# Output projection of a short-convolution layer: the second 1024 columns together, four pairs by seven products, and the first gate on GpSimd

## The chip, the cores and the metric

One core of a Trainium2 chip runs the whole kernel. The metric is the device time of one execution in microseconds (us), the median of several runs. The engines are TensorE (PE; its weight loads are shown as PEld), VectorE (DVE), ScalarE (ACT), GpSimd (Pool) and SyncE (SP), which issues nearly all the loads.

## The reference, cut to what matters

One layer of a short gated convolution with a conditioned norm, in float32, over 256 tokens, a model width D of 2048 and a branch width E of 4096:

```python
h = rmsnorm(x, norm_g[layer])
h, gate = adaln(h, c, ada_w[layer], ada_b[layer])
proj = jnp.einsum('bsd,de->bse', h, w_in)
b_gate, c_gate, v, g = jnp.split(proj, 4, axis=-1)
u = causal_depthwise_conv(c_gate * v, conv_w)
y = b_gate * u * jax.nn.silu(g)
y = jnp.einsum('bse,ed->bsd', y, w_out)
x = x + gate[:, None, :] * y
return rmsnorm(x, final_g)
```

The change lies in the last three lines: y (256 x 4096) times W_out (4096 x 2048), the gated residual and the last norm, whose sum of squares runs over all 2048 columns.

## The kernel before

**Products.** Every float32 operand is split in a high part (rounded, a cast on ACT, `split_hi`, line 352) and a low part (the rest, a subtraction on DVE, `split_lo`, line 357). A product of two blocks is then three TensorE products, high by high, high by low and low by high: `triple` (line 720), 128x512 each in the output projection. The W_in products before it take the first four fifths of the time and are not touched.

**Tiles of the output projection.** y lies transposed: 32 channel tiles of 128 channels, in 16 pairs j, for two halves t of 128 tokens. W_out comes in slabs of 1 MB, `raw_o`, each a DMA issued by SP (`load_o`); three buffers each, used in turn, hold the loads and sums (tag lo), the high parts (tag hi) and the low parts (tag raw). So a load waits for the DVE operation that read the buffer last, and a cast for the PE products that read the high part three tiles ago.

**First 1024 columns.** A slab is two channel tiles (a pair) by 1024 columns. A plain slab takes eight block products for two channel tiles, two column halves and two token halves, 24 TensorE products. Six pairs (`SEVEN`, 10 to 15) take seven block products instead, 21, by sums of blocks: `seven` makes four sums of W_out blocks on DVE (lines 748 to 751), splits three raw blocks (749 and 752) and the four sums, and uses sums of token blocks that `token_forms` prepared. Plain and seven-pairs alternate in the list `order`. Three of the seven results go to extra banks (`p1`, `p6`, `p75`), which `gather` adds to tiles `ends` (called z in the profile); line 798 adds the banks of the plain results. Then `gated` (line 725) multiplies by the gate (731), adds x (732), squares and sums on ACT (733), and multiplies by the norm's weight (734): DVE and ACT alone. In the profile xr, the residual, and fg, the weight, are parts of the tile big.

**Last 1024 columns.** Two blocks of 512 columns (`dc` 2 and 3), each with eight slabs of four channel tiles by 512 columns, 24 products a slab. Block 2 ends in `gated`, and in the sum of squares so far, `part_sum`. For block 3 DVE multiplies the raw slab by the gate first (line 844), and x is put into the bank ahead (line 829), so that its bank ends as the final residual. The last three slabs of block 3 are done for t=0 first; t=1's 36 products of these slabs come last (`late`), so that `finish(0)` (square, root, reciprocal, scaling, four stores) runs beside them. `finish(1)` is the kernel's end. The two token halves of block 3 lie in two PSUM tiles (`both`).

**Order.** A scheduler places each engine's instructions by priorities and an estimate of time; each engine then runs its own list in that order, waiting on semaphores. An instruction that waits holds up all behind it on its engine.

Of the kernel before, what the change touches and what calls it, by code (L numbers as in the profile page):

```python
# [18 lines left out]
NCT = E // P  # L19
TT = T // P  # L20
EPS = 1e-6
# [9 lines left out]
SLOT = 2048  # L31
# [86 lines left out]
def short_conv_layer(ctx: ExitStack, tc: tile.TileContext, x, c, norm_g, ada_w, ada_b, w_in, conv_w, w_out, final_g, out):  # L118
    nc = tc.nc
# [11 lines left out]
    psum = ctx.enter_context(tc.tile_pool(name="psum", bufs=3, space=PSUM))  # L131
# [144 lines left out]
    for t in range(TT):  # L276
        for dh in range(2):
# [94 lines left out]
    def split(raw, n, lo_tag="lo"):  # L372

        return split_lo(raw, n, split_hi(raw, n), lo_tag)
# [22 lines left out]
    for k in range(KT):  # L397
        c_k = silu_c[:, k : k + 1]
        at, gv = first_ada[k], gv0
# [163 lines left out]
    whole = [0] * NCH  # L563
# [27 lines left out]
    def gate(dc):  # L591
        return gates[dc // 2][:, dc % 2, :]
# [35 lines left out]
    EP = 4  # L628
# [80 lines left out]
    LATE = 3  # L709

    def load_o(raw, e0, ne, c0, n):
        nc.sync.dma_start(
            raw.rearrange("p (k f) -> p k f", k=ne),
            w_out[0, e0 * P : (e0 + ne) * P, c0 : c0 + n].rearrange("(k p) f -> p k f", p=P),
        )

    def y_parts(ct, t):
        return [ys[ct // 2][:, ct % 2, h, t * P : (t + 1) * P] for h in range(2)]

    def triple(dst, y, hi, lo, opens=False, ends=False):  # L720

        for i, (a, b) in enumerate(((0, hi), (0, lo), (1, hi))):
            nc.tensor.matmul(dst, y[a], b, start=opens and i == 0, stop=ends and i == 2, skip_group_check=True)  # L723

    def gated(t, c0, n, src, pr, at):


        cs = slice(c0, c0 + n)
        r = xr[:, t, cs]
        g = gates[c0 // 1024].rearrange("p a f -> p (a f)")[:, c0 % 1024 : c0 % 1024 + n]  # L730
        nc.vector.tensor_tensor(out=pr, in0=src, in1=g, op=ALU.mult)
        nc.vector.tensor_tensor(out=r, in0=r, in1=pr, op=ALU.add)
        nc.scalar.activation(pr, r, AF.Square, scale=D**-0.5, accum_out=fsq[:, t, at : at + 1])
        nc.vector.tensor_tensor(out=r, in0=r, in1=fg[:, cs], op=ALU.mult)


    p75 = psum.tile([P, 2, W], F32, tag="mm", name="mm_7")
    wide = [psum.tile([P, 2, W], F32, tag="mm", name="mm_w") for _ in range(TT)]
    p1, p6 = (psum.tile([P, W], F32, tag="sm", name="mm_1", bufs=2) for _ in range(2))

    def seven(j, raw):


        opens, last = j == SEVEN[0], j == SEVEN[-1]
# [3 lines left out]
        nc.vector.tensor_tensor(out=s[:, 0:2], in0=b[:, 1:3], in1=b[:, 0:1].to_broadcast([P, 2, W]), op=ALU.subtract)  # L748
        nc.scalar.copy(bh[:, 1:4], b[:, 1:4])
        nc.vector.tensor_tensor(out=s[:, 2], in0=b[:, 2], in1=s[:, 0], op=ALU.add)  # L750
        all_sums = nc.vector.tensor_tensor(out=s[:, 3], in0=b[:, 3], in1=s[:, 2], op=ALU.subtract)
        low = nc.vector.tensor_tensor(out=bl[:, 1:4], in0=b[:, 1:4], in1=bh[:, 1:4].bitcast(F32), op=ALU.subtract)
# [7 lines left out]
        triple(wide[0][:, 1], y_parts(2 * j + 1, 0), bh[:, 3], bl[:, 3])  # L760
        triple(wide[0][:, 0], f(3), bh[:, 2], bl[:, 2])
# [3 lines left out]
        triple(wide[1][:, 1], y_parts(2 * j + 1, 1), sh[:, 3], sl[:, 3])  # L765

    def gather():
# [9 lines left out]
    order = (0, 1, 10, 2, 11, 3, 12, 4, 13, 5, 14, 6, 15, 7, 8, 9)  # L777
    for n, j in enumerate(order):
        raw = w_tile("lo" if n else "raw", "raw_o")
        load_o(raw, 2 * j, 2, 0, 2 * W)  # L780
        load_ends(n - 4)
        if j in SEVEN:
            seven(j, raw)
            if j == SEVEN[-1]:
                gather()
            continue
        hi, lo = split(raw, SLOT, "raw")
        for t in range(TT):
            for k in range(2):
                for d in range(2):  # L790
                    o = slice((k * 2 + d) * W, (k * 2 + d + 1) * W)
                    triple(
                        wide[t][:, d], y_parts(2 * j + k, t), hi[:, o], lo[:, o],
                        n == 0 and k == 0, j == order[-1] and k == 1,
                    )
    for t in range(TT):
        c = ends[t].rearrange("p h f -> p (h f)")
        nc.vector.tensor_tensor(out=c, in0=wide[t].rearrange("p h f -> p (h f)"), in1=c, op=ALU.add)
# [20 lines left out]
    n_ep = NCT // EP  # L819
    for dc in range(2, 4):  # L820
        dcs = slice(dc * W, (dc + 1) * W)
# [3 lines left out]
        late = []  # L825
        if dc == 3:

            for t in range(TT):
                nc.scalar.copy(po[t], xr[:, t, dcs])

        def out_mm(t, ep, hi, lo):
            for i in range(EP):
                ct = ep * EP + i
                o = slice(i * W, (i + 1) * W)
                triple(po[t], y_parts(ct, t), hi[:, o], lo[:, o], ct == 0 and dc < 3, ct == NCT - 1)

        for ep in range(n_ep):

            raw = w_tile("lo", "raw_o")
            load_o(raw, ep * EP, EP, dc * W, W)  # L840
            if dc == 3:

                raw3 = raw.rearrange("p (k f) -> p k f", k=EP)
                nc.vector.tensor_tensor(
                    out=raw3, in0=raw3, in1=gate(dc).unsqueeze(1).to_broadcast([P, EP, W]), op=ALU.mult
                )
            hi, lo = split(raw, SLOT, "raw")
            out_mm(0, ep, hi, lo)
            if dc == 3 and ep >= n_ep - LATE:
                late.append((ep, hi, lo))  # L850
            else:
                out_mm(1, ep, hi, lo)

        for t in range(TT):
            if t == 1:
                for ep, hi, lo in late:
                    out_mm(1, ep, hi, lo)
            pr = ends[t][:, 0]
            if dc == 2:
                gated(t, dc * W, W, po[t], pr, 1)  # L860
                ps = part_sum[:, t : t + 1]
                nc.vector.reduce_sum(ps, fsq[:, t, 0:2], axis=mybir.AxisListType.X)
                nc.vector.tensor_scalar_add(ps, ps, EPS)
            else:
                nc.scalar.activation(pr, po[t], AF.Square, scale=D**-0.5, accum_out=fsq[:, t, 2:3])
                finish(t)


# [22 lines left out]
```

## Time and profile before

| | us |
|---|---|
| median of 3 runs (lowest, highest) | 906.36 (906.14, 906.43) |
| profiled execution: its time | 907.4 |
| profiled execution: its span | 905.6 |
| first product of the output projection, from the span's start | 727.79 |
| last product's end | 898.01 |

Of the span PE is busy 98%, DVE 73%, ACT 53% and Pool 9%; Pool's work is the turning of gate sums during the W_in part, and nothing in the output projection. The profile is of one execution. A row of the timeline gives start, duration, engine, line, operation, output and inputs (buffer numbers left out), partitions x elements, count, and in brackets how long the engine was idle before and what released it. A row of a group gives the busy time and the mean of one in ns.

### The profile page before, as it was taken

To read this page: it belongs to the slowest core of one execution; us is meant where nothing else is said; L and a number is where in the kernel's file an instruction comes from. 1 tells how busy PE (TensorE), PEld (TensorE's weight loads), DVE (VectorE), ACT (ScalarE), POOL (GpSimd) and SP (SyncE) were. 2 spreads that over 40 slices of the span, in tenths; PEclk is the share of its full clock that TensorE was granted. 3 is DMA by queue.
4 is the path that set the end of the run, shared out by engine and by line. 5 is a ranking of instruction groups with operands and counts; after the bars stand their busy time and mean duration, and the time that the engine had idled before them with its cause. 6 is when DMAs were issued, how large, how long until landed. Compare 5 with 4: busy or idle time off the path is not lost.

```text
span 905.6 us, 16392 instructions
## 1 busy us (share of the span) xinstructions
PE 890.2 (98%) x7009; PEld 852.7 (94%) x7009; DVE 663.9 (73%) x643; ACT 477.8 (53%) x423; POOL 83.6 (9%) x95
## 2 busy tenths in 40 slices
PE   7899999999999999999999999999999999999996
PEld 4899999999999999999999999999999988888885
DVE  5789989988888866765965677565555578887882
ACT  6867866665548766644433444443444445544342
POOL 0000000000000133024224104320000000000000
PEclk9999999999999999999999999999999999999999
DMA  9999999999998588688887788776566486685542
GB/s 310 363 368 363 359 310 353 347 370 356 354 327 289 162 277 244 191 257 246 280 250 239 250 271 267 236 224 191 187 189 193 137 312 201 210 293 186 186 139 94
DMA packets 162665, 235.00 MB, mean 259 GB/s; under 512 B 6804, under 2 KB 105284, under 8 KB 162208
## 3 DMA queue, kind: packets, MB, share of 16 engines
q1 hardware_dynamic: 159456, 226.56, 76.3%
q0 software_dynamic: 3008, 7.34, 2.9%
q8 instruction: 55, 0.90, 0.4%
q14 instruction: 18, 0.15, 0.0%
q10 hardware_dynamic: 128, 0.04, 0.0%
HBM read 224.49 MB, written 2.10 MB: 250 GB/s over the span
## 4 chain that ended last, share of the span: by engine, by line
PE 93%; DMA 3%; SPq 1%; ACT 1%; issue 0%; DVE 0%; ACTq 0%
PE mm_b L491 38%; PE mm_s L491 36%; PE mm_o L723 10%; PE mm_w L723 7%; PE mm L723 2%; DMA at<-in_ada_w_dram 2%; DMA raw_s<-in_sc_w_in_dram 1%; SPq L231 1%; DMA x<-in_x_dram 1%; ACT hi L352 0%; PE tp_g L481 0%; ACT mm_s L524 0%; ACT acc L512 0%; SPq L460 0%; SPq L534 0%
## 5 line engine op out<-in xcount | busy, mean ns | idle before, releaser
L491 PE MATMUL mm_s<-hT,hi 128*128 128x256 f32 x2048 | 350.3, 277 | 1.6 <-ACT hT L328 0.9
L491 PE MATMUL mm_b<-hT,hi 128*128 128x256 f32 x2048 | 348.2, 276 | 0.0
L491 PEld LDWEIGHTS mm_s<-hT,hi 128*128 128x128 f32 x2048 | 308.3, 188 | 2.2 <-ACT hT L328 1.1
L491 PEld LDWEIGHTS mm_b<-hT,hi 128*128 128x128 f32 x2048 | 307.9, 188 | 0.0
L491 PE MATMUL mm_s<-hT,lo 128*128 128x256 f32 x1024 | 282.0, 277 | 0.9 <-DVE lo L357 0.8
L491 PE MATMUL mm_b<-hT,lo 128*128 128x256 f32 x1024 | 282.6, 276 | 0.0
L357 DVE TENSOR_TENSOR lo<-raw,hi 128x2048 fp32r<-128x2048 f32 (+1 forms) x66 | 154.0, 2334 | 101.1 <-ACT hi L352 100.8
L352 ACT CAST hi<-raw 128x2048 fp32r<-128x2048 f32 (+1 forms) x66 | 123.7, 1875 | 192.6 <-PE mm_b L491 150.0
L491 PEld LDWEIGHTS mm_s<-hT,lo 128*128 128x128 f32 x1024 | 191.7, 188 | 1.3 <-DVE lo L357 1.3
L491 PEld LDWEIGHTS mm_b<-hT,lo 128*128 128x128 f32 x1024 | 192.2, 188 | 0.0
L357 DVE TENSOR_TENSOR lo<-raw_s,hi 128x2048 fp32r<-128x2048 f32 (+1 forms) x80 | 149.7, 1877 | 40.2 <-ACT hi L352 39.7
L352 ACT CAST hi<-raw_s 128x2048 fp32r<-128x2048 f32 (+1 forms) x80 | 124.2, 1557 | 60.7 <-PE mm_s L491 49.7
L352 ACT CAST hi<-raw_o 128x2048 fp32r<-128x2048 f32 x26 | 49.6, 1907 | 68.2 <-PE mm_o L723 36.6
L474 DVE SCALAR_TENSOR_TENSOR gv<-at,silu_c,gv 128x512 f32<-128x512 f32 x105 | 78.5, 748 | 6.3 <-DMA at<-in_ada_w_dram 4.7
L357 DVE TENSOR_TENSOR lo<-raw_o,hi 128x2048 fp32r<-128x2048 f32 x26 | 59.5, 2289 | 30.1 <-ACT hi L352 30.1
L723 PE MATMUL mm_o<-hi,y 128*128 128x512 f32 x256 | 78.7, 389 | 0.0
L512 ACT COPY acc<-mm_s 128x1024 f32<-128x1024 f32 x54 | 54.6, 1012 | 39.4 <-PE mm_s L491 39.3
L723 PE MATMUL mm_w<-hi,y 128*128 128x512 f32 x184 | 58.8, 389 | 0.0
L723 PEld LDWEIGHTS mm_o<-hi,y 128*128 128x128 f32 x256 | 48.0, 188 | 9.9
L623 POOL TENSOR_TENSOR gacc<-gacc,z 128x512 f32<-128x512 f32 x28 | 44.0, 1572 | 109.1 <-DMA z<-gacc 109.1
L617 DVE SCALAR_TENSOR_TENSOR gacc<-at_g,silu_c,gacc 128x512 f32<-128x512 f32 x60 | 46.9, 781 | 5.9 <-DMA at_g<-in_ada_w_dram 4.7
L723 PE MATMUL mm_o<-lo,y 128*128 128x512 f32 x128 | 49.5, 389 | 0.0
(145 smaller groups left out, 579.4 us busy)
## 6 DMA issues: line engine op xcount, KB each, us to landing
raw<-in_sc_w_in_dram SPq DMA_DIRECT2D x64, 1024.0 KB, 5.8
raw_s<-in_sc_w_in_dram SPq DMA_DIRECT2D x47, 1024.0 KB, 8.1
raw_o<-in_sc_w_out_dram SPq DMA_DIRECT2D x32, 1024.0 KB, 5.3
at<-in_ada_w_dram SPq DMA_DIRECT2D x114, 256.0 KB, 8.0
raw_s<-in_sc_w_in_dram SPq DMA_DIRECT2D x33, 512.0 KB, 7.0
at_g<-in_ada_w_dram SPq DMA_DIRECT2D x32, 512.0 KB, 7.9
at<-in_ada_w_dram SPq DMA_DIRECT2D x6, 512.0 KB, 9.4
x<-in_x_dram SPq DMA_DIRECT2D x4, 512.0 KB, 6.1
```

The source lines that it names most:

```text
L231: nc.sync.dma_start(at[:, :, s, :], adas[:, j : j + kk, s, 0 : NK0 * P])
L352: nc.scalar.copy(hi[:, :n], raw[:, :n])
L357: nc.vector.tensor_tensor(out=lo[:, :n], in0=raw[:, :n], in1=hi[:, :n].bitcast(F32), op=ALU.subtract)
L474: nc.vector.scalar_tensor_tensor(out=gv, in0=at4[:, i], scalar=c_k, in1=gv, op0=ALU.mult, op1=ALU.add)
L491: mm = last_mm[0] = nc.tensor.matmul(dst, w, h[k], start=begins and left, stop=ends, skip_group_check=True)
L512: nc.scalar.copy(acc[ch, q], bank)
L617: nc.vector.scalar_tensor_tensor(out=ga, in0=at3[:, i, :], scalar=s, in1=ga, op0=ALU.mult, op1=ALU.add)
L623: nc.gpsimd.tensor_tensor(out=ga, in0=ga, in1=turned, op=ALU.add)
L723: nc.tensor.matmul(dst, y[a], b, start=opens and i == 0, stop=ends and i == 2, skip_group_check=True)
```

## The change

The second 1024 columns are done like the first: ten pairs in the order 0, 1, 10, 2, 11, 3, 12, 4, 13, 5, of which 10 to 13 by seven products (`columns`, the former loop as a function, called twice). The remaining twelve channel tiles (`LAST`, three slabs of four) are done one 512-column block at a time: first block 2, then block 3 with the gate multiplied into the slab as before, t=0 first and t=1's 36 products last. Between them the results of the pairs for block 3 are gated, added to x and put into the bank (ACT, line 855). Block 2's gate, squares and `part_sum` come after the last slab's split. The gate of the first 1024 columns runs on Pool instead of DVE. The two token halves of block 3 are the two halves of one PSUM tile, `p75` (mm_7 in the order), which held two of the seven results before.

```diff
-    def gated(t, c0, n, src, pr, at):
+    def gated(t, c0, n, src, pr, at, eng=nc.vector):
...
-        nc.vector.tensor_tensor(out=pr, in0=src, in1=g, op=ALU.mult)
-        nc.vector.tensor_tensor(out=r, in0=r, in1=pr, op=ALU.add)
+        eng.tensor_tensor(out=pr, in0=src, in1=g, op=ALU.mult)
+        eng.tensor_tensor(out=r, in0=r, in1=pr, op=ALU.add)
         nc.scalar.activation(pr, r, AF.Square, scale=D**-0.5, accum_out=fsq[:, t, at : at + 1])
-        nc.vector.tensor_tensor(out=r, in0=r, in1=fg[:, cs], op=ALU.mult)
...
+        eng.tensor_tensor(out=r, in0=r, in1=fg[:, cs], op=ALU.mult)
...
+            places = [(t, k, d) for t in range(TT) for k in range(2) for d in range(2)]
+            if n == 0 and c0:
+                places.sort(key=lambda p: p[2])
...
-        gated(t, 0, 2 * W, c, c, 0)
+        gated(t, 0, 2 * W, c, c, 0, nc.gpsimd)
...
-        both = [psum.tile([P, TT, W], F32, tag="mm", name="mm_o") for _ in range(1 + (dc == 3))]
-        po = [both[-t][:, t] for t in range(TT)]
...
+    halves = [wide_bank("mm_o") for _ in range(2)]
+    p75 = wide_bank("mm_7")
+    LAST = (3, 4, 7)
+    columns(
+        2 * W, (0, 1, 10, 2, 11, 3, 12, 4, 13, 5), SEVEN[0:4],
+        lambda t, d: halves[d][:, t], *extra_banks(), p75, False,
+    )
+    po = [p75[:, t] for t in range(TT)]
...
+    for ep in LAST:
+        raw = w_tile("lo", "raw_o")
+        load_o(raw, ep * EP, EP, 2 * W, W)
+        hi, lo = split(raw, SLOT, "raw")
         for t in range(TT):
...
+            out_mm(halves[0][:, t], t, ep, hi, lo)
+    for t in range(TT):
+        c = ends[t][:, 1]
+        nc.vector.tensor_tensor(out=c, in0=halves[1][:, t], in1=c, op=ALU.add)
+        nc.vector.tensor_tensor(out=c, in0=c, in1=gate(3), op=ALU.mult)
+        nc.vector.tensor_tensor(out=c, in0=c, in1=xr[:, t, 3 * W : 4 * W], op=ALU.add)
+        nc.scalar.copy(po[t], c)
+    late = []
+    for ep in LAST:
...
+        out_mm(po[0], 0, ep, hi, lo)
+        late.append((ep, hi, lo))
+    for t in range(TT):
+        c = ends[t][:, 0]
+        nc.vector.tensor_tensor(out=c, in0=halves[0][:, t], in1=c, op=ALU.add)
+        gated(t, 2 * W, W, c, c, 1)
...
+    for t in range(TT):
+        if t == 1:
+            for ep, hi, lo in late:
+                out_mm(po[1], 1, ep, hi, lo)
+        nc.scalar.activation(ends[t][:, 1], po[t], AF.Square, scale=D**-0.5, accum_out=fsq[:, t, 2:3])
+        finish(t)
```

ACT's queue at the start of the second 1024 columns, before: casts of the slabs of block 2 (hi from raw_o), the copies of x into the banks and the two squares of the first gate, whose input big DVE wrote.

```order
L352 CAST hi_8868<-raw_o_8866 128x2048
L352 CAST hi_8898<-raw_o_8896 128x2048
L352 CAST hi_8928<-raw_o_8926 128x2048
L829 COPY mm_o_9118<-big_8329 128x512
L829 COPY mm_o_9119<-big_8329 128x512
L352 CAST hi_8958<-raw_o_8956 128x2048
L733 ACTIVATE z0_4470,fsq_8330<-big_8329 128x1024
L733 ACTIVATE z1_4471,fsq_8330<-big_8329 128x1024
L352 CAST hi_8988<-raw_o_8986 128x2048
```

The same place now; hi_8872 and hi_8902 are pairs 0 and 1, hi_8933 and hi_8940 pair 10 (raw blocks, sums), hi_8967 pair 2, hi_8998 and hi_9005 pair 11, hi_9032 pair 3 and hi_9063 pair 12.

```order
L352 CAST hi_8872<-raw_o_8870 128x2048
L352 CAST hi_8902<-raw_o_8900 128x2048
L743 CAST hi_8933<-raw_o_8930 128x1536
L352 CAST hi_8940<-sums_o_8932 128x2048
L732 ACTIVATE z0_4470,fsq_8330<-big_8329 128x1024
L352 CAST hi_8967<-raw_o_8965 128x2048
L732 ACTIVATE z1_4471,fsq_8330<-big_8329 128x1024
L743 CAST hi_8998<-raw_o_8995 128x1536
L352 CAST hi_9005<-sums_o_8997 128x2048
```

The two squares (L732, of data that Pool writes) now stand one ahead of pair 2's cast and one between that and pair 11's first cast.

PE's queue between the seventh and the eighth slab of block 2, before: a slab's first product uses the high part, the second the low part.

```order
L723 MATMUL mm_o_8865<-hi_9048,y13_4465 128x512
L723 MATMUL mm_o_8865<-hi_9078,y14_4466 128x512
L723 MATMUL mm_o_8865<-lo_9080,y14_4466 128x512
L723 MATMUL mm_o_8865<-hi_9078,y14_4466 128x512 x2
L723 MATMUL mm_o_8865<-lo_9080,y14_4466 128x512
```

PE's queue now where pair 10 ends and pair 2 begins, with the semaphores that each row waits for:

```order
L722 MATMUL mm_o_8866<-lo_8942,y10_4462 128x512
L722 MATMUL mm_o_8866<-hi_8940,y10_4462 128x512
L722 MATMUL mm_o_8865<-hi_8967,y2_3606 128x512 [waits Activation_49]
L722 MATMUL mm_o_8866<-hi_8967,y2_3606 128x512
L722 MATMUL mm_1_8868<-hi_8998,y11_4463 128x512 [waits Activation_49]
L722 MATMUL mm_o_8865<-lo_8969,y2_3606 128x512 [waits DVE_49]
L722 MATMUL mm_o_8865<-hi_8967,y2_3606 128x512
```

A product with pair 11's high part (hi_8998) now stands ahead of all products with pair 2's low part (lo_8969).

PE's last products, before: t=0 ends in tile mm_o_9118 and t=1 goes on in mm_o_9119, without a wait.

```order
L723 MATMUL mm_o_9118<-hi_9318,y15_4467 128x512 x2
L723 MATMUL mm_o_9118<-lo_9320,y15_4467 128x512
L723 MATMUL mm_o_9118<-hi_9318,y15_4467 128x512
L723 MATMUL mm_o_9119<-hi_9299,y12_4464 128x512 x2
L723 MATMUL mm_o_9119<-lo_9301,y12_4464 128x512
L723 MATMUL mm_o_9119<-hi_9299,y12_4464 128x512
```

And now, where t=0's last slab (hi_9334) ends and the 36 products of t=1 begin:

```order
L722 MATMUL mm_7_8867<-hi_9334,y15_4467 128x512 x2
L722 MATMUL mm_7_8867<-lo_9336,y15_4467 128x512
L722 MATMUL mm_7_8867<-hi_9334,y15_4467 128x512
L722 MATMUL mm_7_8867<-hi_9296,y6_4444 128x512 [waits DVE_49]
L722 MATMUL mm_7_8867<-lo_9298,y6_4444 128x512
L722 MATMUL mm_7_8867<-hi_9296,y6_4444 128x512 x2
```

Both token halves are one tile here, and the first product of t=1 has a wait for DVE.

More of the change, by code (lines that the diff above doesn't have):

```diff
@@ L708, in short_conv_layer @@
     part_sum = const.tile([P, TT], F32, tag="part_sum", name="part_sum")
-    LATE = 3
     def load_o(raw, e0, ne, c0, n):
@@ L775, in gather, with columns, extra_banks, wide_bank @@
         add(ends[1][:, 0], p75[:, 1], ends[1][:, 1])
[L777 to L795, printed above, removed]
+    def columns(c0, order, sevens, bank, p1, p6, p75, whole, loads=None):
+        for n, j in enumerate(order):
+            raw = w_tile("raw" if n == 0 and c0 == 0 else "lo", "raw_o")
+            load_o(raw, 2 * j, 2, c0, 2 * W)
+            if loads:
+                loads(n - 4)
+            if j in sevens:
+                seven(j, raw, bank, p1, p6, p75, j == sevens[0], j == sevens[-1])
+                if j == sevens[-1]:
+                    gather(p1, p6, p75)
+                continue
+            hi, lo = split(raw, SLOT, "raw")
+            places = [(t, k, d) for t in range(TT) for k in range(2) for d in range(2)]
+            if n == 0 and c0:
+                places.sort(key=lambda p: p[2])
+            for t, k, d in places:
+                o = slice((k * 2 + d) * W, (k * 2 + d + 1) * W)
+                triple(
+                    bank(t, d), y_parts(2 * j + k, t), hi[:, o], lo[:, o],
+                    n == 0 and k == 0, j == order[-1] and k == 1 and (whole or d == 1),
+                )
+    def extra_banks():
+        return [psum.tile([P, W], F32, tag="sm", name="mm_1", bufs=2) for _ in range(2)]
+    def wide_bank(name):
+        return psum.tile([P, 2, W], F32, tag="mm", name=name)
+    p75 = wide_bank("mm_7")
+    wide = [wide_bank("mm_w") for _ in range(TT)]
+    columns(
+        0, (0, 1, 10, 2, 11, 3, 12, 4, 13, 5, 14, 6, 15, 7, 8, 9), SEVEN,
+        lambda t, d: wide[t][:, d], *extra_banks(), p75, True, load_ends,
+    )
     for t in range(TT):
@@ new lines, in short_conv_layer @@
+    late = []
+    for ep in LAST:
+        raw = w_tile("lo", "raw_o")
+        load_o(raw, ep * EP, EP, 3 * W, W)
+        raw3 = raw.rearrange("p (k f) -> p k f", k=EP)
+        nc.vector.tensor_tensor(out=raw3, in0=raw3, in1=gate(3).unsqueeze(1).to_broadcast([P, EP, W]), op=ALU.mult)
+        hi, lo = split(raw, SLOT, "raw")
+        out_mm(po[0], 0, ep, hi, lo)
[4 more added lines that the diff above has]
+        gated(t, 2 * W, W, c, c, 1)
+        ps = part_sum[:, t : t + 1]
+        nc.vector.reduce_sum(ps, fsq[:, t, 0:2], axis=mybir.AxisListType.X)
+        nc.vector.tensor_scalar_add(ps, ps, EPS)
```

60 lines of the change are left out of this document (13 added, 47 removed).

## The prediction

> **What bounds the kernel now.** I read the page first, then the chain of waits in order of time, then the busy time by stretch of the last part, then single instructions of VectorE (DVE), GpSimd (Pool) and ScalarE (ACT).
>
> ```profile
> PE 890.2 (98%) x7009; PEld 852.7 (94%) x7009; DVE 663.9 (73%) x643; ACT 477.8 (53%) x423; POOL 83.6 (9%) x95
> 794.16 16.79 PE mm_w L723 x74
> 810.96 87.05 PE mm_o L723 x384
> 898.03 0.70 ACT z L865 x2
> 760.00:780.00 20.00, 20.00 (x89) 16.54 (x89) 17.22 (x13) 9.75 (x6) 0.00 (x0) 1.00 0.65 205
> 860.00:880.00 20.00, 20.00 (x90) 16.57 (x89) 19.01 (x15) 8.25 (x6) 0.00 (x0) 1.00 0.49 157
> ```
>
> The first line is the page's engine table, the next three are the chain, the last two are busy time (PE, weight loads, DVE, ACT, Pool, then granted clock, DMA share, GB/s). PE is the bound and has no gap: the 384 products of the two column blocks that the change rewrites took 87.05 us, 226.7 ns each. A product removed there is worth 0.227 us, if PE is never made to wait. Behind PE stands DVE: 17.22 of 20 us while pairs by seven products alternate with plain pairs, so it has 2.8 us in 20 to spare.
>
> **Products.** Four pairs lose one group of three products each: 12 x 0.2267 = **-2.7 us**. This holds in any order; the order has 738 products after the W_in part instead of 750.
>
> **DVE work added and removed.** A seven-pair costs DVE these operations where a plain slab has the first alone:
>
> ```profile
> L357 DVE TENSOR_TENSOR lo<-raw_o,hi 128x2048 fp32r<-128x2048 f32 x5 | 11.5, 2292 | 7.1 <-ACT hi L352 7.1
> L752 DVE TENSOR_TENSOR lo<-raw_o,hi 128x1536 fp32r<-128x1536 f32 x5 | 8.8, 1751 | 0.0
> L748 DVE TENSOR_TENSOR sums_o<-raw_o 128x1024 f32<-128x1024 f32 x5 | 6.1, 1218 | 0.0
> L750 DVE TENSOR_TENSOR sums_o<-raw_o,sums_o 128x512 f32<-128x512 f32 x5 | 3.5, 692 | 0.2
> ```
>
> That is 1.22 + 2 x 0.69 + 1.75 + 2.29 = 6.6 us a pair. By itself it is hidden: the first 1024 columns run just so with PE full (the 760 to 780 row). The five gate multiplications fewer (eight slabs become three) free time that nobody waited for. Taking the six operations of the first gate off DVE gains nothing either: they stood beside plain slabs, which ask 2.29 us of DVE for every 24 products, 5.44 us, of PE. Cost zero, if DVE is not held up. It is, by the next edit.
>
> **First gate on Pool.** Six operations on 128x1024 go to Pool, at the moment when DVE gets its fullest stretch. The trace shows what a Pool operation does to a DVE operation that reads two SBUF tiles:
>
> ```profile
> 330.41 2.86 POOL L623 TENSOR_TENSOR gacc<-gacc,z 128x512 f32<-128x512 f32 x1 [5.63 <-DMA z<-gacc]
> 329.82 2.29 DVE L357 TENSOR_TENSOR lo<-raw_s,hi 128x2048 fp32r<-128x2048 f32 x1 [3.15 <-ACT hi L352]
> 332.55 2.87 DVE L357 TENSOR_TENSOR lo<-raw_s,hi 128x2048 fp32r<-128x2048 f32 x1 [0.44 <-ACT hi L352]
> 402.72 1.29 POOL L623 TENSOR_TENSOR gacc<-gacc,z 128x512 f32<-128x512 f32 x1 [5.88 <-DMA z<-gacc]
> 403.26 2.89 DVE L357 TENSOR_TENSOR lo<-raw,hi 128x2048 fp32r<-128x2048 f32 x1 [1.14 <-ACT hi L352]
> 488.49 1.30 POOL L623 TENSOR_TENSOR gacc<-gacc,z 128x512 f32<-128x512 f32 x1 [2.14 <-DMA z<-gacc]
> 488.47 0.69 DVE L677 TENSOR_TENSOR z<-mm_b,z 128x512 f32<-128x512 f32 x1 [1.32 <-PE mm_b L491]
> ```
>
> Pool's 512 elements take 1.29 us alone. Beside a DVE operation it took 2.86: that one ended at 332.11, and Pool 1.16 later, at 333.27. The next DVE operation, started at 332.55, took 2.87, 0.58 over its 2.29; so did the one at 403.26 (0.60 over). They take turns, and the later one waits. The pair at 488 did not disturb each other: there DVE reads one operand from PSUM. For 1024 elements I take 2.4 us alone and 2.25 after a wait, just under twice the 512 row (the fixed part is paid once); the nearest row above is the mean of 1572 ns over 28 such operations, waits included, twice that being 3.1. The Trainium skill, "GPSIMD Engine Reference", section Instruction dispatch, gives about 2.5 cycles an element for two inputs at 1.2 GHz; that estimates 2.1 us, and by it the sum would be some 0.7 us lower.
>
> Pool's six turns are 13.8 us of time taken from DVE. Bounds of what PE waits for it: zero, if Pool ran only in DVE's gaps; 13.8 less DVE's spare 3.9 in 28 us, 9.9, if DVE had no lead. Between them I go step by step, T being the time from the first product of the second columns, with the durations above and these:
>
> ```profile
> L352 ACT CAST hi<-raw_o 128x2048 fp32r<-128x2048 f32 x26 | 49.6, 1907 | 68.2 <-PE mm_o L723 36.6
> 752.50 1.48 ACT L749 CAST hi<-raw_o 128x1536 fp32r<-128x1536 f32 x1 [1.55 <-DMA raw_o<-in_sc_w_out_dram]
> 818.29 1.05 ACT L733 ACTIVATE z<-big 128x1024 f32<-128x1024 f32 x1
> 809.71 2.52 DVE L798 TENSOR_TENSOR z<-mm_w,z 128x1024 f32<-128x1024 f32 x2
> raw_o<-in_sc_w_out_dram SPq DMA_DIRECT2D x32, 1024.0 KB, 5.3
> ```
>
> DVE ends a sum begun earlier and adds the first columns' banks (PSUM, so not held) from 0.6 to 3.0. Pool gates t=0 until 4.3; pair 10's low part (1.75) therefore runs 4.2 to 5.9, Pool's gate of t=1 5.9 to 8.1, its first addition 8.2 to 10.6, DVE's low part of pair 10's sums 10.4 to 12.7, Pool's second addition 12.7 to 14.9. In ACT's queue the squares, which wait for Pool, stand between the casts, which PE waits for; so ACT squares t=0 at 10.6, casts pair 2 until 13.6, then waits for Pool: square of t=1 15.0 to 16.1, cast of pair 11 until 17.6. PE needs that cast after 71 products (pairs 0, 1 and 10 and two of pair 2), at 16.1: **1.5 us**. DVE's first sum of pair 11 ends at 16.0, Pool's third operation on t=0 takes 16.0 to 18.3, pair 2's low part comes at 20.4; PE needed it at 17.8: **2.6**. Pool's last takes until 22.6, pair 11's sums and low parts end at 25.6 and 28.1; PE is there 33 products after 20.4, at 27.9: **0.2**. The load for pair 12 could start only at 25.6, lands 5.3 later, is cast at 32.4; PE asks 11 products after 28.1, at 30.6: **1.8**. Together **+6.1 us**. From there Pool is done, and pairs 12 and 13 run as their like in the first columns did, with PE full.
>
> **The last sixteen microseconds.** Before, t=0 and t=1 of the last block end in two PSUM tiles; now both are halves of one tile, mm_7. In the order PE's first product of the late t=1 therefore waits for DVE, whose last use of that tile is the multiplication of t=0's result in finish. PE has nothing else queued. The same steps in before, where PE worked beside them:
>
> ```profile
> 893.05 0.60 ACT L865 ACTIVATE z<-mm_o 128x512 f32<-128x512 f32 x1 [9.38 <-PE mm_o L723]
> 893.75 1.28 ACT L806 ACT_TABLE_LOAD   x1
> 895.05 0.29 ACT L806 ACTIVATE fs<-fsq,part_sum 128x1 f32<-128x1 f32 x1
> 895.38 0.16 DVE L807 RECIPROCAL fs<-fs 128x1 f32<-128x1 f32 x1 [9.38 <-ACT fs L806]
> 895.98 0.74 DVE L812 SCALAR_TENSOR_TENSOR big<-mm_o,fs,big 128x512 f32<-128x512 f32 x1
> ```
>
> 893.05 to 896.72 is 3.67 us. Add 0.16 (a product ends 0.39 after its start, the next would start after 0.23) and about 0.5, since block 2's squares and part_sum, formerly done 30 us earlier, now stand just ahead on ACT and DVE: **+4.3 us** (3.8 to 4.8). The low parts of the three slabs before it come 0 to 0.5 us ahead of PE by the same counting; I take nothing. The output tail after t=1 is unchanged.
>
> **Sum.** -2.7 + 6.1 + 4.3 = +7.7 us. The profiled execution took 907.4 (span 905.6 and 1.8 around it), so 915.1; it lies 1.0 over the median of 906.36, so **914.1 us** for the median. A difference of 0.2% (1.8 us) is about what a measurement of this kernel can tell from none.
>
> **Rivals.** *Pool gives way.* If Pool's turns came only in DVE's gaps and its squares were moved by nothing else, the 6.1 fall away and the two other terms leave +1.6: 908.0, no difference that counts. It decides where the sum of the first waits is under 0.2 us, so if Pool's second addition ends before T = 13.5, so that the square (1.1) and pair 11's cast (1.5) still come before 16.1, and no turn holds DVE. For it: Pool did wait at 330.41. Against it: the rows at 332.55 and 403.26, where DVE waited. The Trainium skill, "SBUF — State Buffer", section Who interferes with whom, has the order of issue decide who is blocked, for the whole instruction; the 332.55 row agrees. Chance 0.05.
>
> *The clock falls in the pause.* PE idles about 4.1 us before the late products.
>
> ```profile
> 900.00:902.00 2.00, 0.00 (x0) 1.00 0.71 270
> 902.00:904.00 2.00, 0.00 (x0) 0.75 0.76 254
> 4.25 5.04 PE L258 MATMUL tp_idle<-ones,ident 128*128 128x512 f32 x6
> 9.41 4.58 PE L258 MATMUL tp_idle<-ones,ident 128*128 128x512 f32 x10
> ```
>
> Here the granted clock was whole until 902 and 0.75 on average over the next two, so it fell near 903, 5.0 us after the last product's end at 898.01 (810.96 + 87.05). At the start six products took 0.84 us each, the next ten 0.46: about 5 us of slow running, worth 5 x (1 - 0.46/0.84) = 2.3 us. With it 916.4. The rows leave 0.9 us of margin, but from one pause of one run; the fall may come earlier. The Trainium skill, "TensorE: Matmul & The Clock Gate", Part 1, has a free-running window of about 3.4 us, idle once for half the clock; by it a pause of 4.1 would be hit in some runs. Chance 0.2.
>
> *Pool is dearer.* At 3.1 us an operation six turns hold DVE 4.8 longer, nearly all of it ahead of PE's waits: 918.9. Chance 0.1. *The tile wait costs nothing*, if PE were let go by the square: 909.8, chance 0.05. Faster by something unseen: 0.02. The forecast: 0.58.
>
> **Range and chances.** The forecast's own range is 911.5 (stalls of 3.5) to 916 (stalls of 7.5, pause 4.8). The slow clock reaches 917 to 918. 910.0 to 918.0 leaves out the giving way, the free tile wait, the faster case and most of the dear Pool, under 0.2. Faster 0.02, same 0.05 (the giving way), slower 0.93.
>
> **What would show it.** Right: products without gaps up to the second columns; then PE idle just before the first products of pairs 2, 11 and 12, with DVE operations of 2.29 us that take 3 to 4.6 and Pool operations of 2.4 that take 3 to 4.5; a pause of about 4.3 us between the 36 last products and those before, released by DVE. Wrong: DVE durations unchanged beside Pool; PE waits put down to loads alone; late products that follow at once; other PE gaps in the last three slabs.

## The result, and the profile after

The changed kernel took 918.7 us (median of 4 runs, 917.83 to 919.75), the kernel before 906.26 (4 runs on the same chip, 906.14 to 906.43): a ratio of 1.0138, 95% interval 1.0125 to 1.015. It is 1.4% slower: the way was forecast, but 12.4 us came where 7.7 were forecast, and the time lies 0.7 us above the range. The profiled execution took 919.53, with a span of 917.7 against 905.6. Two of the four runs took 917.8 and 917.9, two 919.5 and 919.8; the account below is of the one with a trace, 919.53. One execution of the kernel with both parts undone (below) took 1511.9 us at a mean granted clock of 0.56, and its ratio is taken from the other nine.

PE's busy time hardly shows it. The engine table of the profile's page:

```profile
PE 891.7 (97%) x6997; PEld 852.4 (93%) x6997; DVE 677.1 (74%) x660; ACT 483.9 (53%) x428; POOL 108.9 (12%) x101
```

The 12 products are gone (7009 to 6997), yet PE is counted as busy for longer than the 890.2 us of before: where its clock is halved (below), 13 products fill 4 us. What PE waited for from 800 us on (us in total, times, longest); the same list of the kernel before, up to its last product, is empty:

```profile
PE mm L722 <- DVE big L823: 4.2, 1, 4.2
PE mm L722 <- ACT hi L743: 4.0, 2, 2.0
PE mm_o L722 <- DVE lo L357: 2.4, 1, 2.4
PE mm L722 <- DVE lo L357: 0.2, 1, 0.2
```

The waits stand where the prediction put them. Counted from one product's start to the next, less the 0.227 us of a step (and with 0.11 that the first step behind a wait is longer at the full clock), they are 0.5 (pair 10's sums), 2.2 (pair 11's cast), 2.7 (pair 2's low part) and 2.3 us (pair 12's cast), 7.65 together, and 4.4 for the pause before the late products. Pool, DVE and ACT at that place, each in order of time (start, duration, in square brackets the idle time before and what ended it):

```profile
812.67 6.26 POOL L730 TENSOR_TENSOR z<-z,gate 128x1024 f32<-128x1024 f32 x2 [215.31 <-DVE z L809]
818.90 6.82 POOL L731 TENSOR_TENSOR big<-big,z 128x1024 f32<-128x1024 f32 x2
825.68 7.71 POOL L733 TENSOR_TENSOR big<-big 128x1024 f32<-128x1024 f32 x2
```

```profile
823.50 3.31 DVE L742 TENSOR_TENSOR sums_o<-raw_o 128x1024 f32<-128x1024 f32 x1
826.73 4.44 DVE L357 TENSOR_TENSOR lo<-raw_o,hi 128x2048 fp32r<-128x2048 f32 x1
831.10 2.85 DVE L744 TENSOR_TENSOR sums_o<-raw_o,sums_o 128x512 f32<-128x512 f32 x1
```

```profile
825.76 1.06 ACT L732 ACTIVATE z<-big 128x1024 f32<-128x1024 f32 x1 [1.46 <-POOL big L731]
826.82 1.45 ACT L743 CAST hi<-raw_o 128x1536 fp32r<-128x1536 f32 x1
843.60 1.47 ACT L743 CAST hi<-raw_o 128x1536 fp32r<-128x1536 f32 x1 [3.50 <-DMA raw_o<-in_sc_w_out_dram]
```

Pool's six operations last 20.8 us with hardly a break, and DVE beside them takes 3.31, 4.44 and 2.85 us for what takes 1.22, 2.29 and 0.69 alone. In ACT's queue the square (825.76) waits for Pool's sum, and the cast that PE wants stands behind it. The last row is the late load of pair 12.

What the sum did not have is in the busy time by stretch; the column behind the five engines is PE's granted clock:

```profile
828.00:832.00 4.00, 1.27 (x3) 0.87 (x4) 4.00 (x2) 0.27 (x1) 4.00 (x2) 0.91 0.00 0
832.00:836.00 4.00, 4.00 (x13) 3.11 (x13) 3.97 (x3) 1.22 (x1) 1.40 (x1) 0.66 0.83 262
898.00:900.00 2.00, 0.47 (x1) 0.47 (x2) 1.31 (x3) 1.36 (x3) 0.00 (x0) 0.90 0.15 58
900.00:902.00 2.00, 2.00 (x6) 1.54 (x6) 0.00 (x0) 0.00 (x0) 0.00 (x0) 0.50 1.07 382
902.00:904.00 2.00, 2.00 (x9) 1.58 (x8) 0.00 (x0) 0.00 (x0) 0.00 (x0) 0.75 0.27 96
```

The clock fell to half twice. A mean of 0.90 over 2 us is 0.4 us at half, so one fall began at 899.6, and with 2.0 and 1.0 us in the next two rows it lasted 3.4. In the same way the other ran from 831.3 for 3.4 us: 0.7 us of the first row, 2.7 of the second. Products then follow each other every 0.43 us instead of 0.227. In the chain of waits, the 36 late products:

```profile
899.53 10.08 PE mm L722 x36
```

The last of them starts 9.68 us after the first; at the full clock 35 steps are 7.93, so the fall there cost 1.7 (3.4 us at half can't cost more; the expectations below have 1.9, from 36 steps against the last product's end). The first fall, counted from start to start behind 831.2, cost 1.7 as well. The whole account of the projection: -2.7 + 7.65 + 1.7 + 4.4 + 1.7 = +12.75; its measured length, from the first product's start to the last one's end, went from 170.4 (727.63 to 898.00) to 183.1 us (726.51 to 909.60), +12.7.

### The profile page after: what moved, and what is told of

The parts are those of the page before. It is cut to its first block, busy times and chain, and to the rows that moved or that the text cites. A ratio compares the mean times of both kernels' runs of the same rounds, so it can differ in the third digit from the quotient of the medians.

```text
span 917.7 us, 16411 instructions
## 1 busy us (share of the span) xinstructions
PE 891.7 (97%) x6997; PEld 852.4 (93%) x6997; DVE 677.1 (74%) x660; ACT 483.9 (53%) x428; POOL 108.9 (12%) x101
## 4 chain that ended last, share of the span: by engine, by line
PE 87%; DVE 5%; DMA 4%; ACT 2%; issue 1%; SPq 1%; ACTq 0%; DVEq 0%
PE mm_b L491 38%; PE mm_s L491 35%; PE mm_w L722 7%; PE mm L722 4%; PE mm_o L722 2%; DVE lo L357 2%; DMA at<-in_ada_w_dram 2%; DMA raw_s<-in_sc_w_in_dram 1%; SPq L231 1%; DMA raw_o<-in_sc_w_out_dram 1%; DVE raw_o L861 1%; ACT hi L352 1%; DMA x<-in_x_dram 1%; DVE sums_o L744 0%; PE tp_g L481 0%
## 5 line engine op out<-in xcount | busy, mean ns | idle before, releaser
L357 DVE TENSOR_TENSOR lo<-raw_o,hi 128x2048 fp32r<-128x2048 f32 x22 | 52.4, 2385 | 17.8 <-ACT hi L352 17.8
L623 POOL TENSOR_TENSOR gacc<-gacc,z 128x512 f32<-128x512 f32 x28 | 50.3, 1797 | 121.2 <-DMA z<-gacc 121.2
L352 ACT CAST hi<-raw_o 128x2048 fp32r<-128x2048 f32 x22 | 42.0, 1907 | 42.5 <-PE mm_o L722 10.2
L621 POOL DMA_DIRECT2D z<-gacc x28 | 15.8, 563 | 334.2 <-DVE acc L558 284.5
L722 PE MATMUL mm_o<-hi,y 128*128 128x512 f32 x160 | 51.5, 396 | 0.0
L722 PEld LDWEIGHTS mm_w<-hi,y 128*128 128x128 f32 x184 | 34.5, 188 | 7.2
```

What stands on the lines that cost most here:

```text
L352: nc.scalar.copy(hi[:, :n], raw[:, :n])
L357: nc.vector.tensor_tensor(out=lo[:, :n], in0=raw[:, :n], in1=hi[:, :n].bitcast(F32), op=ALU.subtract)
L621: nc.gpsimd.dma_start(turned[0 : P - away], ga[away:P])
L623: nc.gpsimd.tensor_tensor(out=ga, in0=ga, in1=turned, op=ALU.add)
```

## The experiments

The theory after this result: Pool's gate holds up DVE, and through its squares ACT, where DVE is fullest; the shared tile makes the pause; each long idle of PE costs a fall of the clock besides. The rivals: the four pairs by seven products and their loads are dear whoever does the gate; the pause has another cause; the clock falls at its own times, whatever PE does. The first four runs undo one part, the other, both, and do one alone.

**The gate back on DVE.**

```diff
-        gated(t, 0, 2 * W, c, c, 0, nc.gpsimd)
+        gated(t, 0, 2 * W, c, c, 0)
```

> The changed kernel with its first gate back on DVE (six operations of 128x1024); the single PSUM tile for the last block stays. Theory (Pool's gate holds up DVE and ACT where DVE is fullest, 7.65 us of waits before products and one fall of the clock worth 1.7 us): the waits of 2.2, 2.7 and 2.2 us go, DVE's own 6 x 1.2 us of gate leave at most one wait of 0 to 2 us in their place, the pause of 4.4 us before the 36 late products stays and the clock falls there: 906.3 - 2.7 + 1.6 + 4.4 + 1.9 = 911.5 us (909.5 to 913). Rival (the waits come from the four pairs by seven products and their late loads, whoever does the gate): the waits stay, 917 us or more.

913.68 us (913.17 to 914.13), 1.008 of before (1.0065 to 1.0095): 5.0 us come back, and the time is 0.7 us above the range of the theory. PE's waits of this kernel:

```profile
PE mm L722 <- DVE big L823: 4.1, 1, 4.1
PE mm_o L722 <- DVE lo L357: 1.5, 1, 1.5
PE mm L722 <- ACT hi L743: 1.3, 1, 1.3
PE mm L722 <- DVE lo L357: 0.5, 1, 0.5
```

No fall of the clock before the pause (1.00 from 820 to 840 us), and the waits shrink from 7.65 to 4.0 us, not to 1.6. What stays is more than the theory's one wait and less than the rival's: DVE's own gate (813.41 to 825.0) now stands ahead of the low part of pair 2, which starts at 826.06, and the load of pair 12 waits for that low part, since it needs its raw tile.

**Two tiles for the last block.**

```diff
-    po = [p75[:, t] for t in range(TT)]
+    po = extra_banks()
```

> The changed kernel with the last block's two token halves in two one-bank PSUM tiles instead of two halves of one tile; the gate stays on Pool. Theory (the 36 late products wait for DVE to read the other half of their tile): the pause of 4.4 us goes and the clock's fall behind it, the waits of 7.65 us and one fall stay, and the end of the first half is drawn later by up to 1 us: 906.3 - 2.7 + 7.65 + 1.7 + 0.5 = 913.5 us (911.5 to 914.5), no wait over 0.5 us in front of the late products. Rival (the pause has another cause, the last transfers or the change of ACT's table): the pause stays, 918.7 us.

913.32 us (912.75 to 913.7), 1.0076 (1.0061 to 1.0091). All that PE still waits for:

```profile
PE mm_o L722 <- DVE lo L357: 2.4, 1, 2.4
PE mm L722 <- ACT hi L743: 2.0, 1, 2.0
```

The pause and the fall behind it are gone, 5.4 us together; the pause was the tile's. The first fall is twice as long here as in the changed kernel, 6.8 us from 829.8 to 836.6, though the two waits ahead of it are the same:

```profile
820.00:830.00 10.00, 6.51 (x27) 4.50 (x25) 9.97 (x3) 5.47 (x6) 10.00 (x4) 0.99 0.08 34
830.00:840.00 10.00, 8.99 (x28) 7.19 (x29) 8.38 (x5) 2.89 (x2) 3.18 (x1) 0.67 0.58 189
```

The late cast of pair 12 is not waited for: PE came to it that much later. A fall can thus hide a later wait.

**Both undone.** The two edits above together.

> The changed kernel with the gate on DVE and two PSUM tiles. Theory: of the +12.4 us only the 12 products fewer (-2.7), one wait of about 1.6 us and a tail longer by about 1 us are left: 906.2 us (905 to 908), the clock full through the last 185 us. Rival (the four pairs by seven products are dear in themselves): 910 us or more.

908.08 us, 1.002 (1.001 to 1.0029). The parts add up: 918.7 - 5.0 - 5.4 = 908.3. The clock is full throughout the projection. What holds it above the 903.6 of the products alone is 4.0 us of waits like those of the gate on DVE, and a tail of 8.5 us behind the last product instead of 7.6. SyncE's queue, which issues the loads, from 810 to 842 us:

```profile
SPq L711 <- DVE lo L357: 24.2, 3, 11.6
SPq L711 <- DVE lo L746: 7.8, 2, 5.2
SPq L711 <- DMA raw_o<-in_sc_w_out_dram: 1.5, 1, 1.5
```

The loads wait for DVE's low parts, not for the memory: the pairs by seven products are not dear for their transfers, but for what stands on DVE ahead of them.

**The kernel before with its first gate on Pool.**

```diff
-        gated(t, 0, 2 * W, c, c, 0)
+        gated(t, 0, 2 * W, c, c, 0, nc.gpsimd)
```

> The kernel before with nothing but its first gate moved to Pool. Theory (the port's contention costs only where DVE is full; in the plain stretch of the kernel before DVE and ACT have slack): 906.3 us, at most 908, Pool's six operations taking 2.4 to 4.4 us each and DVE's beside them 2.5 to 4.5 us as in the changed kernel, without waits over 1 us before products. Rival (six operations on Pool cost their 6 to 8 us wherever they stand): 912 to 915 us.

906.42 us, 0.9999 of before (0.9989 to 1.0008). DVE beside Pool is stretched here too, and PE waits for nothing:

```profile
809.82 6.82 POOL L731 TENSOR_TENSOR z<-z,gate 128x1024 f32<-128x1024 f32 x2 [212.85 <-DVE z L798]
```

```profile
817.17 3.98 DVE L357 TENSOR_TENSOR lo<-raw_o,hi 128x2048 fp32r<-128x2048 f32 x1 [2.79 <-ACT hi L352]
```

2.79 us of idle ahead of an operation that takes 1.7 longer: the plain slabs have the room. The same move costs nothing in one stretch and about 5 us in another. In this kernel and in all of the above the projection's first product starts between 726.2 and 726.6 us, so what they differ by lies in the projection and behind it.

**The pause filled.** To the changed kernel, products that nothing uses are added in the pause:

```diff
         if t == 1:
+            spare = extra_banks()[0]
+            for i in range(WARM):  # WARM = 15
+                mm = nc.tensor.matmul(spare, y_parts(0, 0)[0], late[-1][1][:, 0:W], ...)
+                tc.add_manual_dep(mm.ins, done.ins.name, after, reason="in the pause")
             for ep, hi, lo in late:
```

> The changed kernel (one tile, gate on Pool) with 15 products of 0.227 us into a free PSUM bank after the last product of the first token half: the 4.4 us pause is filled with 3.4 us of work that nothing uses, and PE waits some 0.7 to 1 us as late as before. Theory (behind the pause the clock falls for 3.4 us and the 16 products there take 1.9 us more): the fall there goes, the pause's own 4.4 us stay, 918.7 - 1.9 = 916.8 us (915 to 917.3), and PE's clock is full in the stretch of the late products. Rival (the time after the pause is set by what follows, or the clock falls at its own times whatever PE does): 918.7 us.

916.28 us (915.66 to 917.14), 1.0112 (1.0098 to 1.0126): 2.4 less than the changed kernel, whose profile had 1.7 in that fall; here the 36 late products take 8.5 us (898.88 to 907.37) instead of 10.1. The wait that is left, and two stretches of busy time:

```profile
898.88 0.50 PE L722 MATMUL mm<-hi,y 128*128 128x512 f32 x1 [0.81 <-DVE big L824]
```

```profile
832.00:836.00 4.00, 4.00 (x11) 3.10 (x10) 3.97 (x3) 1.44 (x1) 1.18 (x1) 0.50 0.83 262
899.00:904.00 5.00, 5.00 (x22) 4.11 (x23) 0.00 (x0) 0.00 (x0) 0.00 (x0) 1.00 0.58 213
```

The late products still start when DVE lets them, but at the full clock; the earlier fall, whose idle was left as it was, is still there (6.8 us long in this profile, from 829.4). Whether the clock falls thus follows PE's idleness.

**The squares behind the cast.** ACT's two squares of the first gate are emitted after pair 11's cast (casts[-1]) and depend on it. The multiplication by the norm's weight, which follows each square, goes with them; on Pool it starts at 825.62, as before (825.68).

```diff
+        sq = nc.scalar.activation(pr, r, AF.Square, scale=D**-0.5, accum_out=...)
+        if not at:
+            tc.add_manual_dep(sq.ins, casts[-1].ins.name, after, reason="behind this cast")
```

> The changed kernel with ACT's two squares of the first gate put behind the cast of the second stage's pair 11, in front of which they stood; the gate is on Pool as before. Theory (the lock alone sets the wait: the low part of pair 2 on DVE is late beside Pool's last operations, and the wait for the cast, 2.2 us, is only an earlier part of the same idle): the wait for ACT's cast goes, the wait for DVE's low part grows from 2.7 to about 4.5 us, 918.3 us (916.5 to 919.5). Rival (ACT's queue behind the squares is a cost of its own): 916.5 us or less, the wait for the low part staying at 2.7 us.

919.4 us (918.12 to 919.93), 1.0144 (1.0129 to 1.016). The cast now begins at 822.72 instead of 826.82, and PE waits once at this place:

```profile
831.15 0.79 PE L724 MATMUL mm_o<-lo,y 128*128 128x512 f32 x1 [4.70 <-DVE lo L357]
```

From start to start 4.9 us, as much as 2.2 and 2.7 together. ACT's queue behind Pool was real and cost nothing of its own: the low part of pair 2 was as late anyway. Pair 12's wait (2.4 us from start to start) and the pause (4.4) stay.

**All mended.** Gate on DVE, two tiles, the squares behind the cast, and the last two thirds of the late products behind the last product of t=0. With the squares go DVE's two multiplications by the norm's weight, so that pair 2's low part starts at 822.88 instead of 826.06 with the gate on DVE alone. Of the edits the last:

```diff
-            for ep, hi, lo in late:
-                out_mm(po[1], 1, ep, hi, lo)
+            for (ep, hi, lo), d in zip(late, [None, 2, 2]):
+                out_mm(po[1], 1, ep, hi, lo, done[d] if d is not None else None)
```

> The changed kernel with its first gate on DVE, two one-bank tiles for the last block, ACT's squares of the gate behind the cast of pair 11, and the last two thirds of the late products behind the last product of the first half. Theory (nothing is left but the 12 products fewer): the waits of 0.6, 1.7 and 1.6 us of the run with both parts undone go (the low part of pair 2 earlier by two operations of the gate, and with it the load of pair 12, which waits for it), its tail is shorter by 1 us: 906.3 - 2.7 = 903.6 us (902.8 to 905). Rival (pairs by seven products at this place lose to the transfers what they save): 906 us or more, with waits for raw_o's transfers before pair 12.

904.55 us (11 runs, 903.6 to 905.39) against 906.16 (15 runs): 0.9982 (0.9973 to 0.9991), 1.6 us faster than the kernel before. All of PE's waits from 800 us on, and the stretch that had idled for 4.7 us:

```profile
PE mm L724 <- DVE lo L357: 0.3, 1, 0.3
```

```profile
812.00:834.00 22.00, 22.00 (x98) 18.09 (x97) 21.35 (x16) 11.20 (x9) 0.00 (x0) 1.00 0.51 172
```

DVE is busy for 21.35 of the 22 us, with the gate, and PE never stops. Of the 2.7 us 1.6 arrive. What is missing lies in two gaps of 0.4 and 0.6 us from start to start and in a tail of 8.0 us for 7.6.

**Pool's operations alone.** The mended kernel with six additions on Pool that nobody waits for; the output's last 1024 columns are scaled by them.

```diff
+    spare = const.tile([P, 1], F32, tag="spare", name="spare")
+    idle = fg[:, 2 * W :]
+    prior = nc.gpsimd.tensor_copy(out=spare, in_=ends[1][:, 0, 0:1])
+    for _ in range(6):
+        op = nc.gpsimd.tensor_tensor(out=idle, in0=idle, in1=idle, op=ALU.add)
```

> The kernel of the run beside this one (gate on DVE, two tiles, squares behind the cast, late products in order) plus six Pool additions of 128x1024 in place on columns of final_g, started after the second half's sum of the first stage; nothing waits for them before the last stage, and the output's last 1024 columns are scaled by them, so that it isn't the reference's. Theory (Pool's operations hold up DVE by the port that they share): Pool's six take 3 to 4.4 us each, DVE's beside them 2.5 to 4.5 us in place of 1.2 to 2.3, with DVE's gate in the same stretch PE waits 8 to 12 us and the clock falls once: 903.7 + 11.6 + 1.8 = 917 us (912 to 919). Rival (only waits for Pool's results cost): 903.7 us.

944.2 us (943.56 to 944.67), neither theory's number. From the first product of the projection to its last 181.0 us went by, against 168.8 in the mended kernel: 12.2 more, where the theory had 13.4. But the first product came at 752.7 us instead of 726.0, and everything before it was nearly 4% slower from the start, 27 us that no work on Pool at 840 us can cause. The one other thing new was the tile spare. Once more with a larger one:

```diff
-    spare = const.tile([P, 1], F32, tag="spare", name="spare")
+    spare = const.tile([P, 16], F32, tag="spare", name="spare")
```

> The run with Pool's six additions once more, its one small extra tile made 64 bytes per partition instead of 4: before, every tile of the pools allocated behind it lay 32 bytes further (the cast tile hi at 64352 instead of 64320), here 64 bytes. As before the last 1024 output columns are scaled by the additions. Theory (the 32 bytes cost the 26 us outside the projection, Pool's additions only the 12.2 us inside it, 181.0 against 168.8): the first product of the projection at about 725.8 us again, 904.6 + 12.2 = 916.8 us (915 to 918.5). Rival (the additions or the small tile cost the 26 us in another way): 944 us.

945.04 us (944.23 to 945.53): a tile of 64 bytes does the same, so it is not the 32 bytes in particular. The small tile without the additions, added to the mended kernel:

```diff
+    spare = const.tile([P, 1], F32, tag="spare", name="spare")
+    nc.gpsimd.tensor_copy(out=spare, in_=ends[1][:, 0, 0:1])
```

> The kernel with all mended plus a tile of 4 bytes per partition and one copy of a 128x1 column into it on Pool, no additions: the tiles of the later pools lie 32 bytes further. Theory (the matmuls of 128x256 take 281 ns in place of 276 where their operands are off by 32 bytes): the products of the two input projections 4% slower, the first product of the output projection at about 752.5 us, 904.6 + 26.7 = 931 us (929 to 933). Rival (the additions were the cause): 904.6 us (903.5 to 906).

934.09 us (933.89 to 934.5), 1.0305 (1.0288 to 1.0322): the additions are not the cause. And the additions without the tile, their starting copy going into part_sum, which exists:

```diff
+    prior = nc.gpsimd.tensor_copy(out=part_sum[:, 0:1], in_=ends[1][:, 0, 0:1])
```

> The kernel with all mended plus Pool's six additions of 128x1024 on columns of final_g, started by a copy into a column that exists already, so that no tile moves; the last 1024 output columns are scaled by the additions. Theory (the moved tiles cost the time outside the projection, Pool's port the 12.2 us inside it): 904.6 + 12.2 = 916.8 us (915 to 918.5), the first product of the projection at about 725.8 us. Rival (Pool's operations cost the time outside too): 944 us. Rival (work on Pool that nobody waits for is free): 904.6 us.

915.29 us (913.47 to 916.08), 1.0097 (1.0082 to 1.0112): 10.7 over the mended kernel, at the lower end of the first theory. This is the lock, the turns that Pool and DVE take at SBUF, by itself; Pool and DVE in order of time, and PE's waits:

```profile
814.90 18.65 POOL L825 TENSOR_TENSOR big<-big 128x1024 f32<-128x1024 f32 x6
```

```profile
824.99 3.98 DVE L357 TENSOR_TENSOR lo<-sums_o,hi 128x2048 fp32r<-128x2048 f32 x1
829.00 2.80 DVE L754 TENSOR_TENSOR sums_o<-raw_o 128x1024 f32<-128x1024 f32 x1
831.72 3.98 DVE L357 TENSOR_TENSOR lo<-raw_o,hi 128x2048 fp32r<-128x2048 f32 x1
```

```profile
PE mm L724 <- DVE lo L357: 6.2, 2, 5.4
PE mm_o L724 <- DVE lo L357: 2.3, 1, 2.3
```

Nobody wants anything of Pool, and PE waits 8.5 us for DVE. The clock falls twice beside it, for 3.4 us each from 828.6 and 835.4, and these falls are part of the 10.7:

```profile
829.00:832.00 3.00, 2.98 (x7) 2.40 (x8) 3.00 (x2) 0.00 (x0) 2.92 (x2) 0.50 0.00 0
832.00:833.00 1.00, 1.00 (x5) 0.83 (x5) 1.00 (x1) 0.00 (x0) 1.00 (x1) 0.99 0.00 0
836.00:839.00 3.00, 3.00 (x8) 2.34 (x9) 3.00 (x4) 0.00 (x0) 0.00 (x0) 0.52 0.72 199
```

The low part that takes 2.29 us takes 3.98, the sum of 1.22 takes 2.80: each is longer by 1.6 to 1.7 us, the turn that Pool has first. The Trainium skill, "SBUF — State Buffer", section Who interferes with whom, has a DVE instruction with two SBUF inputs contend with one of GpSimd that reads SBUF; these rows agree.

**A larger tile.** The mended kernel plus a tile of 128 bytes per partition, cleared once by DVE.

```diff
+    spare = const.tile([P, 32], F32, tag="spare", name="spare")
+    nc.vector.memset(spare, 0.0)
```

> The kernel with all mended plus a tile of 128 bytes per partition that DVE clears once (no copy on Pool): the cast tile hi lies at 64448, 128 bytes further; 32 and 64 bytes further, at 64352 and 64384, the 128x256 products took 281 to 282 ns in place of 276. Theory (what counts is the place within 128 bytes, which is the same again): 904.6 us (903.5 to 906), 276 ns. Rival (any move of the tiles, or what stands behind them, costs the 27 us): 930 us or more.

912.15 us (911.23 to 913.1), 1.0064 (1.0047 to 1.0081): between the two. More on this at the end.

## Why the prediction was right or wrong

**Products.** 12 fewer, 2.7 us: the count is right; the mended kernel, nearest to showing them alone, has 1.6 of it.

**Pool's gate.** The place and order of the waits were right: pair 11's cast behind the squares, pair 2's low part, pair 12's load. In size +6.1 was forecast and 7.65 came: 2.2 for 1.5, 2.7 for 2.6, 2.3 for 1.8, and 0.5 where 0.2 stood at another place. Pool took 2.40 us alone, as chosen, and up to 4.4 where DVE's long operation went first. Two readings of these terms were off. The 1.5 us for ACT's queue are no term: moved out of the way, they came back in the next. And not all of it was Pool's: with the gate on DVE 4.0 us of waits stay, because the prediction's "nothing gained by taking it off DVE" looked at the plain slabs of before, while in the new order DVE's gate too stands ahead of pair 2's low part and so of pair 12's load. Pool instead of DVE cost 5.0 us by the medians; the two profiles have 3.65 of waits and 1.7 of the first fall of the clock.

**The pause.** +4.3 forecast, 4.4 measured, released by DVE's L823, gone with two tiles: right, in size and in cause.

**The clock is the step that failed.** It stood as a rival with a chance of 0.2 and 2.3 us, for the pause alone; the profile had two falls worth 3.4 together, the main part of what its account has above the forecast (12.75 for 7.7; the waits have 1.55 of it, the pause 0.1). The error was to read a threshold from one row (a fall 5.0 us after the last product in the kernel before) and to see 0.9 us of margin in a pause of 4.1; a fall cost 1.7 and not 2.3. With 4.1 to 4.4 us of idle in that place the clock fell in every profile that has the pause unfilled: the changed kernel, the gate on DVE, the squares behind the cast. And the prediction added up 1.5 and 2.6 us of idle before pairs 11 and 2 without asking what the clock does there: with 2.0 and 2.4 us, and one product between them, it fell as well. In the run with Pool's additions and the tile of 64 bytes it fell (at 865.3) behind a wait of 2.3 us from start to start, while one of 2.4 with the squares behind the cast (up to 845.0) left it whole, and so did the changed kernel's last, 2.2; the length of a single wait does not decide. The Trainium skill, "TensorE: Matmul & The Clock Gate", Part 1, has a free-running window of 3413 ns; the two falls are 68.3 us apart, 20 such windows, and each lasted 3.4 us, so the trace agrees. The page asks for one idle window; the 3.4 us up to the fall at 831.3 held one product of 0.49 us, so here the measurement decides: a window idle for the most part was enough.

The traces say how much. Counted in steps of 3.413 us forward and back from a fall of the same profile, the windows right ahead of the falls of all profiles (twelve before the last products, and one behind them in each profile) held 2.0 to 3.4 us of idle PE, and no window that no fall followed held more than 1.9. The nearest two: with Pool's additions and no tile, 832.03 to 835.44 had its last product end at 833.4, 2.0 us idle, and the clock fell; in the changed kernel 841.56 to 844.97 had 1.9 us idle, and it did not. The kernel before fits too: its products ended at 898.0, the window up to 899.57 had 1.6 us idle, the next was all idle, and the fall came at its end, 903.0. So the 5.0 us that the prediction read as a threshold were the place of the windows. That place also sets how long a fall lasts: the slow clock stayed for a second window where PE idled 1.2 us or more of the first one (two tiles, the filled pause, the first run with Pool's additions) and ended after one where it idled 0.5 or less. This is read off these profiles, from ends of products that are modelled, and no run was made to test it.

The other three executions of the changed kernel had mean granted clocks of 0.992, 0.992 and 0.991 against 0.994 for the profiled one; a window more at half is 0.002. They probably had longer falls, and yet two were 1.7 us faster; no trace of them shows what the falls hid.

**The other rivals.** Pool does not give way (its additions alone cost 10.7 us, falls of the clock included), it is not dearer (2.40 alone), and the tile's wait is not free. The range fell 0.7 us short because the clock was put beside the forecast, once, and not twice on top of stalls of 7.65, which lie just above the forecast's own 7.5.

## What to carry to other kernels

Before work is moved to an engine that takes turns with the busy one, as Pool does with DVE, look at the stretch in which it will run and not at the one from which it is taken: the same six operations cost nothing where DVE idled 2.8 us between casts and about 5 us where it was full. Where PE will idle for 2 us or more within 3.4 us, neighbouring waits added up, price a fall of the clock on top (here 1.7 us for each 3.4 us at half), with a chance: whether it comes depended on where the windows lay. Two buffers that end at different times do not belong in one tile if somebody reads one while the other is still written; and a wait that vanishes when its cause is moved may only show the next one, so judge it by the sum.

## What the runs showed of the hardware beside this

A tile of 4 bytes per partition, set down ahead of the pools, made the kernel 3% slower from its first microseconds on; the copy on Pool that came with it did not, since the run with the copy and no tile kept its first product of the projection at 726.8 us. The 128x256 products of the mended kernel and of the one with the small tile (duration in ns, least, median and most; first and last start):

```profile
L491 PE MATMUL mm_b<-hT,hi x2048: 276/276/277, 377.9 to 725.8; 128*128 128x256 f32 x187
```

```profile
L491 PE MATMUL mm_b<-hT,hi x2048: 280/280/283, 390.9 to 752.5; 128*128 128x256 f32 x187
```

All 2048 take 280 ns or more instead of 276, at a granted clock of 1.00; from the first to the last of these starts the time per product grew by 3.9% (361.6 us for 347.9). By the expectations above, the cast tile hi moved by 32 bytes here, by 64 with the tile of 64 bytes, whose median was 282 ns, and by 128 with the tile of 128 bytes, which has 276 again, though that run still lost 7.6 us (in the profiles 4.5 before the projection and 3.4 in it). So it matters where the tiles lie, and 128 bytes further the products themselves are as fast as before; what rule is behind it, and what the rest of the 7.6 us is, stays open.
